# A hybrid layer on one core: another order of the mixers, compressed scores from a split key, and 128-column blocks without padding

## The chip, the core and the metric

The kernel runs on one core of a Trainium2 chip. The metric is the device time of one execution in microseconds; the kernel before took 1316.21 us as the median of 3 runs (1316.2 to 1316.97). Times in the profile are those of one profiled execution.

## What is computed

One transformer layer over a sequence of 1024 tokens of width 1024, in float32: an RMS norm, one input projection, four kinds of mixers on its columns, a gain per group, an output projection with a residual, a second norm and a gated feed-forward network.

```
proj = rms_norm(x) @ w_in
o_a = nsa_mixer(...)                  # 4 heads: compressed, selected and window attention, gated
o_b = gate_b * conv(gate_c * u)       # 256 channels, 3 taps
o_c = stick_breaking_attention(...)   # 4 heads: softplus, a reverse running sum, exp
o_d = dilated_attention(...)          # 4 heads: three dilations, mixed by their log-sums
groups = rms_norm([o_a, o_b, o_c, o_d]) * g_out
x = x + groups @ w_out
x = x + (silu(h2 @ w_gate) * (h2 @ w_up)) @ w_down      # h2 = rms_norm(x)
```

In the compressed branch the keys are reduced to 63 tokens, and a query block is scored against all 63 (`einsum('bhqd,bnd->bhqn', qi, kc)`).

## The kernel before

**Number format.** A float32 operand of a matmul is held as two tiles of type fp32r, a high part and the rest ("hi" and "lo", `whi` and `wlo`, `XH` and `XL`); a product is three matmuls (`mm3`, lines 240 to 243), or two where the high and low parts of one operand are stacked in the 128 rows. Where an operand stays plain float32 (the compressed scores, line 693, and transposes), one matmul is issued; the trace has two records for each such score matmul.

**Stages.** The normalized rows are transposed into `XH` and `XL`; keys and values are compressed (lines 454 to 508); then come the mixers, each of the letters in `ORDER` (line 44) being one piece of the program: `n0 n1` the two head pairs of the first mixer (`attn_nsa`, line 635), `c0 c1` the halves of the convolution (`conv`, line 806), `pd0 pd1` and `ps0 ps1` the projections for the dilated and stick-breaking attention (lines 379 and 385), `d0 d1` and `s0 s1` these attentions (`attn_dil`, line 738; `attn_stick`, line 775), and `g` (`gains`, line 832), which reads seven of the eight 128-row groups of mixed results back and scales them into `MH` and `ML`. The eighth group, that of the last attention, goes there straight from `finish` (line 622). After that `out_half` (line 899) multiplies by `w_out`: for rows 512 to 1023 with the seven groups alone, the eighth being added at the end (line 975), for rows 0 to 511 with all eight. The feed-forward network follows (lines 1042 to 1215), with products in a scheme of seven instead of eight.

**Attention.** Queries go in blocks of 128 rows (`qt`); scores are formed by `qk_pair` (line 513) over the keys up to the diagonal, in chunks of up to 512 columns. `chunks` (line 535) gives each chunk its width and the width it is run at: `res.append((c, w, max(256, w)))`, so that a chunk of 128 columns is run as 256 and half of the result is not used. A dilated or stick-breaking block then passes VectorE (the minimum with a bias, line 545, or the cap, lines 791 and 793, and the running sum, line 799), ScalarE and, in the stick-breaking case, GpSimd (line 801), before `pv` (line 568) transposes the probabilities on TensorE (line 580), takes them out of PSUM as hi and lo (`evac_T`, lines 564 and 565) and multiplies them with the values (lines 584 and 585). Two query blocks share these last matmuls, 256 columns; the last key block belongs to the second query block alone, and its matmul is filled up to 256 with 128 columns of zeros that stand at the head of each of the four buffers of `pt_pair` (line 550).

**What sets the order.** The program is built twice. The first time a planner (`_traced`, `_planned`) walks all instructions up to the last pools with a cost for each (`_duration`, line 1489) and starts on each engine the ready instruction that is first in the program, moved up by a lead; leads stand in a table by engine, tile tag and tile (`LEADS`, line 1244). The second time each engine's instructions, and the slots of the tiles, are pinned to that plan (`fix_order`, line 1768). So work of a later piece runs beside an earlier one, as far as tiles allow: the ring `QK` of smq has 10 tiles of 4 KB per partition (the keys and queries of the first mixer hold 8; each `pd` or `ps` takes 5), and the tag `V` has 2.

Of the kernel before, what the change touches and what calls it, by code (L numbers as in the profile page):

```python
# [9 lines left out]
F32 = mybir.dt.float32  # L10
# [6 lines left out]
T = 1024  # L17
# [26 lines left out]
ORDER = "n0 n1 c0 pd0 d0 pd1 d1 ps0 s0 c1 ps1 g s1".split()  # L44
# [7 lines left out]
def hybrid(ctx, tc, pools, x, gmix, wa1, wa2, wkv, wcv, wd, wc, bgate, gcols, pe, w1, w2,  # L52
# [393 lines left out]
    kcT = cst.tile([128, 64], F32, name="kcT")  # L446
# [7 lines left out]
    for z, src in ((0, KK), (1, VV)):  # L454
# [40 lines left out]
        if z == 0:  # L495
# [9 lines left out]
            nc.scalar.activation(kcT[:, :63], tp[:, :63], AF.Copy, scale=gsc[:, 1:2])  # L505
# [42 lines left out]
    PT = []  # L548

    def pt_pair():  # L550

        if not PT:
            for i in range(2):
                z = [sm.tile([128, 640], F32R, tag=f"pt{i}{c}", bufs=1, name=f"pt{c}") for c in "hl"]
                for t in z:
                    nc.gpsimd.memset(f(t[:, 0:128]), 0.0)
                PT.append(z)
        PT.reverse()
        return PT[0]

    def evac_T(tp, n):
        ph, pl = pt_pair()
        c = slice(128, 128 + n)
        nc.scalar.activation(ph[:, c], tp[:, :n], AF.Copy)  # L564
        nc.vector.tensor_tensor(pl[:, c], tp[:, :n], f(ph[:, c]), op=OP.subtract)  # L565
        return ph, pl

    def pv(o, items, first=True, last=True):

        n = len(items)  # L570
        for g in range(0, n, 2):
            tp = Ttile()
            grp = items[g:g + 2]
            cols = (128, 384)
            ps = [p for it in grp for p in it[:2]]
            if grp[-1][0] is None:
                cols = (256, 0)
                ps = [ps[3], ps[0], ps[1]]
# [22 lines left out]
    def finish(k8, c0, n, m, tmp, bank=None):  # L601
        nc.scalar.activation(tmp, m, AF.Square)
        for h in range(0, n, 512):
# [3 lines left out]
            if SQ == 0 or (SQ == 1 and k8 == 5):  # L607
                nc.tensor.matmul(ps[:, :w], f(blk1r), tmp[:, c], start=True, stop=True)
            else:
                sh, sl = (whl("sh"), whl("sl")) if bank else (z[:, 128:640] for z in pt_pair())  # L610
# [10 lines left out]
        if k8 == 5:  # L621
            gain(5, m, c0 // 512, slice(c0 % 512, c0 % 512 + n))
            return
# [11 lines left out]
    def attn_nsa(hp, Q):  # L635
# [7 lines left out]
        for qt in range(NT):  # L643
# [48 lines left out]
            for h in range(2):  # L692
                nc.tensor.matmul(ps[h][:, :63], f(Q[h][:, qc]), kcT[:, :63], start=True, stop=True)
# [8 lines left out]
            nc.tensor.matmul(o[:, :256], vcHL, ph[:, 128:384], start=True, stop=False)  # L702
            nc.tensor.matmul(o[:, :256], vcHL, pl[:, 128:384], start=False, stop=False)
# [118 lines left out]
    def gain(k, m, h, c):  # L822
        hi, lo = (z[:, k, c] for z in MS[h])
        if k != 5 and GP >> h & 1:
# [7 lines left out]
    def gains():  # L832
        flush_stores()
        MS.extend((xtile("MH"), xtile("ML")) for _ in range(2))
        if GH:
            for h in (1, 0):
                for k in (0, 1, 2, 3, 6, 7, 4):
# [3 lines left out]
        else:  # L841
            for k in (0, 1, 2, 3, 6, 7, 4):
# [6 lines left out]
    for o in ORDER:  # L849
        if o[0] == "c":  # L850
# [5 lines left out]
        else:  # L856
# [6 lines left out]
            else:  # L863
                if not i:
                    tri_ = [diag_mask()]
                attn_stick(i, *done["ps" + o[1]])
    att.close()
# [72 lines left out]
    K7 = ((0, 1, 2, 3, 6, 7, 4), ((0, 2), (2, 2), (6, 2), (4, 1)))  # L940
# [5 lines left out]
    out_half(0, (0, 1, 2, 3, 6, 7, 4, 5), ((0, 2), (2, 2), (6, 2), (4, 2)), range(0, D, 256))  # L946
# [13 lines left out]
    w5 = []  # L960
    for h in range(2):
        raw = wraw()
        nc.sync.dma_start(raw[:, :512], wout[:, 5, h * 512:(h + 1) * 512])
        hi, lo = whl("whi"), whl("wlo")
        split(hi[:, :512], lo[:, :512], raw[:, :512])
        w5.append((hi[:, :512], lo[:, :512]))
# [4 lines left out]
    for t in range(4, NT):  # L971
        c = slice(t % 4 * 128, t % 4 * 128 + 128)
        for h in range(2):
            ps = PRt()
            mm3(ps, tuple(z[:, 5, c] for z in MS[1]), w5[h], True, True)
# [115 lines left out]

    for i in range(NF // 2):
# [152 lines left out]
    "ACT B22 B": -430,  # L1245
    "ACT QK St": -535,
    "ACT QK ckh": -277,
    "ACT QK ckl": -96,
    "ACT QK cqh": -569,
    "ACT QK cql": -698,  # L1250
    "ACT QK dkh": -727,
    "ACT QK dkl": -1057,
    "ACT QK dqh": 921,
    "ACT QK dql": -192,
    "ACT QK er": -998,
    "ACT QK fw": -1315,
    "ACT QK ksh": 211,
    "ACT QK kt": 12,
    "ACT QK kwh": 629,
    "ACT QK q01h": -828,  # L1260
    "ACT QK q01l": -338,
    "ACT QK q23h": -732,
    "ACT QK q23l": 33,
# [6 lines left out]
    "ACT S4 S": 368,  # L1270
    "ACT S4 cm": 459,
    "ACT S4 kv": 1132,
    "ACT S4 wa": -119,
    "ACT T3 T": 286,
    "ACT T4 T": -754,
    "ACT V VA": -39,
    "ACT V VC": -861,
    "ACT V VD": -499,
    "ACT V bhl": -98,
    "ACT V yc": 297,  # L1280
    "ACT W R": -15,
    "ACT X B": 658,
    "ACT X MH": 74,
    "ACT X T": -744,
    "ACT X XH": -406,
    "ACT gt gt": 677,
    "ACT hss hss": 866,
    "ACT kcT kcT": -217,
    "ACT ll ll": -294,
    "ACT otmp otmp": 1259,  # L1290
    "ACT otmp tk": 109,
    "ACT pt0h pth": -106,
    "ACT pt1h pth": -55,
    "ACT pth pth": -53,
    "ACT pth sh": 6,
    "ACT ss ss": -37,
    "ACT tk raw": -981,
    "ACT tk rawk": 332,
    "ACT tk sq": -645,
    "ACT tk vraw": -340,  # L1300
    "ACT vcHL vcHL": 1499,
    "ACT whl c": -827,
    "ACT whl p": -826,
    "ACT whl sh": 66,
    "ACT whl u": -1188,
    "ACT whl whi": 97,
    "DVE B22 B": -223,
    "DVE MO MO": -290,
    "DVE QK St": -351,
    "DVE QK ckr": -103,  # L1310
    "DVE QK cqh": -1540,
    "DVE QK cql": 425,
    "DVE QK dkr": 192,
    "DVE QK dqh": -544,
    "DVE QK dql": -245,
    "DVE QK er": -357,
    "DVE QK fw": -2071,
# [554 lines left out]
```

## Time and profile before

| | before |
|---|---|
| median of 3 runs | 1316.21 us |
| the profiled execution | 1314.44 us |
| its span, first to last instruction | 1312.7 us |
| TensorE matmul busy | 1281.9 us |
| VectorE busy | 987.8 us |
| ScalarE busy | 703.9 us |
| GpSimd busy | 659.6 us |

The sum of the prediction is made against the profiled execution, 1314.44 us, which is 1.8 us below the median; 1.7 us of it lie outside of the span. Busy time of TensorE counts from each matmul's start to its modelled end, and neighbours overlap; the spacing of starts tells more than the durations. PEld is the load of the stationary operand, which runs beside the matmuls.

### The profile page before, as it was taken

How to read it: one execution, taken by the hardware profiler on the slowest of the kernel's cores; microseconds unless marked ns; L12 is line 12 of the kernel's file. 1: busy time of each engine (PE TensorE's matmuls, PEld its weight loads, DVE VectorE, ACT ScalarE, POOL GpSimd, SP SyncE). 2: the span in 40 equal slices, each digit the busy share in tenths (PEclk: the TensorE clock that was granted, in tenths of full speed). 3: DMA queues.
4: the chain of work that ended last, by engine and by line, in shares of the span. 5: the costliest groups of instructions: out<-in, count | busy, mean ns of one | idle time of the engine just before them, and what ended most of it. 6: DMA issues, size and time to landing. Idle time of an engine off the chain costs nothing.

```text
span 1312.7 us, 20252 instructions
## 1 busy us (share of the span) xinstructions
PE 1281.9 (98%) x7041; PEld 1089.3 (83%) x7041; DVE 987.8 (75%) x1792; ACT 703.9 (54%) x1437; POOL 659.6 (50%) x492
## 2 busy tenths in 40 slices
PE   8999999999999999999999999999999999999998
PEld 7988889999788887898987888888888887887886
DVE  5868888898878865885577979677765677499963
ACT  5658688777768875576554333332333335523440
POOL 6454256443214463786882446344543344564755
PEclk9999999999999999999999999999999999999999
DMA  7340021121312025533554454233232239862434
GB/s 249 93 125 12 5 79 40 41 75 28 100 49 60 11 66 148 165 120 117 161 190 144 156 189 153 84 118 120 101 107 73 93 124 321 283 198 73 145 97 152
DMA packets 90550, 153.04 MB, mean 117 GB/s; under 512 B 10128, under 2 KB 35728, under 8 KB 90448
## 3 DMA queue, kind: packets, MB, share of 16 engines
q1 hardware_dynamic: 89888, 149.92, 35.5%
q0 software_dynamic: 560, 1.84, 0.4%
q8 instruction: 55, 0.90, 0.3%
q14 instruction: 47, 0.39, 0.1%
HBM read 111.08 MB, written 36.44 MB: 112 GB/s over the span
## 4 chain that ended last, share of the span: by engine, by line
PE 79%; DVE 10%; DMA 4%; ACT 3%; issue 2%; POOL 1%; SPq 0%; DVEq 0%; POOLq 0%; ACTq 0%
PE PRp L241 9%; PE PRp L242 9%; PE PRp L243 9%; PE Tp L580 4%; PE PRp L1062 4%; PE PRp L1061 4%; PE PRp L1060 4%; PE SPp L518 2%; PE Op L585 2%; PE Tp L1060 2%; PE SPp L1060 2%; PE SPp L1061 2%; PE SPp L1062 2%; PE Tp L1061 2%; PE Tp L1062 2%
## 5 line engine op out<-in xcount | busy, mean ns | idle before, releaser
L108 POOL TENSOR_TENSOR wlo<-raw,whi 128x512 fp32r<-128x512 f32 x94 | 133.4, 1425 | 89.4 <-ACT whi L107 70.0
L1049 POOL TENSOR_TENSOR fw<-fraw,fw 128x512 fp32r<-128x512 f32 x50 | 72.0, 1441 | 137.9 <-ACT fw L1048 111.0
L565 DVE TENSOR_TENSOR ptl<-Tp,pth 128x512 fp32r<-128x512 f32 (+2 forms) x172 | 102.3, 605 | 26.8 <-ACT pth L564 23.7
L1119 DVE TENSOR_TENSOR fw<-sraw,fw 128x512 fp32r<-128x512 f32 x73 | 89.1, 1240 | 34.7 <-ACT fw L1118 34.6
L1048 ACT ACTIVATE fw<-fs 128x512 fp32r<-128x512 f32 x88 | 52.9, 629 | 112.9 <-DVE fs L1039 84.9
L564 ACT ACTIVATE pth<-Tp 128x512 fp32r<-128x512 f32 (+2 forms) x172 | 89.3, 530 | 44.3 <-PE Tp L580 30.2
L580 PE MATMUL Tp<-ident,S 128*128 128x128 f32 x552 | 101.5, 273 | 3.2 <-DVE ptl L565 3.1
L1119 POOL TENSOR_TENSOR hw<-bB,hw 128x512 fp32r<-128x512 f32 x55 | 80.4, 1476 | 46.6 <-ACT hw L1118 46.5
L241 PE MATMUL PRp<-XH,whi 128*128 128x512 f32 x224 | 90.5, 404 | 0.3 <-DVE VD L374 0.3
L242 PE MATMUL PRp<-XL,whi 128*128 128x512 f32 x224 | 90.0, 402 | 0.0
L243 PE MATMUL PRp<-XH,wlo 128*128 128x512 f32 x224 | 89.6, 400 | 0.0
L1049 DVE TENSOR_TENSOR fw<-fs,fw 128x512 fp32r<-128x512 f32 x88 | 76.4, 901 | 14.2 <-ACT fw L1048 14.0
L660 POOL TENSOR_SCALAR S<-S,ll 128x640 f32<-128x640 f32 (+7 forms) x32 | 53.8, 1680 | 63.1 <-DVE ll L658 14.4
L107 ACT ACTIVATE whi<-raw 128x512 fp32r<-128x512 f32 x102 | 63.0, 619 | 33.7 <-PE PRp L242 13.3
L580 PEld LDWEIGHTS Tp<-ident,S 128*128 128x128 f32 x552 | 69.1, 141 | 10.3 <-DVE ptl L565 3.9
L241 PE MATMUL PRp<-whi,MH 128*128 128x256 f32 (+1 forms) x248 | 71.3, 291 | 1.0 <-ACT MH L827 0.6
L242 PE MATMUL PRp<-wlo,MH 128*128 128x256 f32 (+1 forms) x248 | 71.3, 289 | 0.0
L243 PE MATMUL PRp<-whi,ML 128*128 128x256 f32 (+1 forms) x248 | 70.5, 289 | 0.0
L801 POOL TENSOR_TENSOR S<-S,R 128x128 f32<-128x128 f32 (+7 forms) x32 | 47.5, 1484 | 42.9 <-DVE R L799 42.9
L1048 ACT ACTIVATE fw<-fraw 128x512 fp32r<-128x512 f32 x50 | 31.3, 627 | 68.5 <-PE PRp L1062 35.0
L1118 ACT ACTIVATE hw<-bB 128x512 fp32r<-128x512 f32 x62 | 38.8, 628 | 53.0 <-PE Op L243 24.6
L1039 POOL TENSOR_TENSOR u<-u,p 128x512 f32<-128x512 f32 x22 | 32.5, 1478 | 64.7 <-DVE u L1039 43.9
(472 smaller groups left out, 4504.2 us busy)
## 6 DMA issues: line engine op xcount, KB each, us to landing
fraw<-in_wgate_dram SPq DMA_DIRECT2D x22, 512.0 KB, 3.9
fraw<-in_wup_dram SPq DMA_DIRECT2D x22, 512.0 KB, 4.3
bB<-in_wdown_dram SPq DMA_DIRECT2D x44, 256.0 KB, 4.3
sraw<-hS SPq DMA_DIRECT2D x44, 256.0 KB, 2.7
raw<-in_wout_dram SPq DMA_DIRECT2D x30, 256.0 KB, 2.8
hS<-s SPq DMA_DIRECT2D x30, 256.0 KB, 2.2
sraw<-hA SPq DMA_DIRECT2D x29, 256.0 KB, 3.9
xt<-in_x_dram SPq DMA_DIRECT2D x8, 512.0 KB, 9.6
```

The costliest lines, as they stand in the source:

```text
L108: (lo or nc.gpsimd).tensor_tensor(dst_lo, raw, f(dst_hi), op=OP.subtract)
L241: nc.tensor.matmul(ps, a[0], b[0], start=first, stop=False)
L242: nc.tensor.matmul(ps, a[0], b[1], start=False, stop=False)
L243: nc.tensor.matmul(ps, a[1], b[0], start=False, stop=last)
L564: nc.scalar.activation(ph[:, c], tp[:, :n], AF.Copy)
L565: nc.vector.tensor_tensor(pl[:, c], tp[:, :n], f(ph[:, c]), op=OP.subtract)
L580: nc.tensor.transpose(tp[:, i * 128:(i + 1) * 128], p, ident)
L1049: eng.tensor_tensor(wt[:, 1, :], a, f(wt[:, 0, :]), op=OP.subtract)
L1060: nc.tensor.matmul(ps, wt[:, 0, c], bh[:, k, :], start=k == 0, stop=False)
L1061: nc.tensor.matmul(ps, wt[:, 0, c], bl[:, k, :], start=False, stop=False)
L1062: nc.tensor.matmul(ps, wt[:, 1, c], bh[:, k, :], start=False, stop=k == 3)
L1119: eng.tensor_tensor(wt[:, 1, :], raw, f(wt[:, 0, :]), op=OP.subtract)
```

## The change

- `ORDER` becomes `n0 c0 n1 c1 ps0 s0 ps1 s1 pd0 d0 pd1 g d1`. The last attention, whose group goes straight into `MH` and `ML`, is `d1` instead of `s1`; the numbers 5 and 7 of the groups change places accordingly in `finish`, `gain`, `gains`, `K7` and the group that is added at the end.
- The compressed keys become two fp32r tiles, and a compressed score is two matmuls of 64 columns instead of one float32 matmul of 63.
- `chunks` runs a chunk at its own width. `pv` multiplies the last key block at 128 columns; the zeros and their four memsets go, and `pt_pair` is a plain ring of 2 per tag.
- The planner has another table of leads, now by tile and by tile and stage (`pools.mark()` marks the beginning of each piece), and counts 400 ns instead of 60 for each DMA issue of SP. So the order on every engine, up to the last pools, is another one, and the SP and POOL queues with it.

```diff
-ORDER = "n0 n1 c0 pd0 d0 pd1 d1 ps0 s0 c1 ps1 g s1".split()
+ORDER = "n0 c0 n1 c1 ps0 s0 ps1 s1 pd0 d0 pd1 g d1".split()
...
-    kcT = cst.tile([128, 64], F32, name="kcT")
+    kcT = [cst.tile([128, 64], F32R, name=f"kcT{c}") for c in "hl"]
+    for z in kcT:
+        nc.gpsimd.memset(f(z[:, 63:64]), 0.0)
...
-            nc.scalar.activation(kcT[:, :63], tp[:, :63], AF.Copy, scale=gsc[:, 1:2])
+            nc.scalar.activation(kcT[0][:, :63], tp[:, :63], AF.Copy, scale=gsc[:, 1:2])
+            nc.vector.scalar_tensor_tensor(kcT[1][:, :63], tp[:, :63], gsc[:, 1:2], f(kcT[0][:, :63]),
+                                           op0=OP.mult, op1=OP.subtract)
...
-            res.append((c, w, max(256, w)))
+            res.append((c, w, w))
...
-                z = [sm.tile([128, 640], F32R, tag=f"pt{i}{c}", bufs=1, name=f"pt{c}") for c in "hl"]
-                for t in z:
-                    nc.gpsimd.memset(f(t[:, 0:128]), 0.0)
-                PT.append(z)
-        PT.reverse()
-        return PT[0]
+        return [sm.tile([128, 512], F32R, tag=f"pt{c}", bufs=2, name=f"pt{c}") for c in "hl"]
...
-            if grp[-1][0] is None:
-                cols = (256, 0)
-                ps = [ps[3], ps[0], ps[1]]
+            ps = [p for it in grp for p in it[:2] if p is not None]
...
-                c = slice(cols[i], cols[i] + 256)
-                nc.tensor.matmul(o[:, :256], v, ph[:, c], start=first and g + i == 0, stop=False)
-                nc.tensor.matmul(o[:, :256], v, pl[:, c], start=False, stop=last and g + i == n - 1)
+                b = 256 if grp[i][0] is not None else 128
+                c = slice(i * 256, i * 256 + b)
+                nc.tensor.matmul(o[:, 256 - b:256], v, ph[:, c], start=first and g + i == 0, stop=False)
+                nc.tensor.matmul(o[:, 256 - b:256], v, pl[:, c], start=False, stop=last and g + i == n - 1)
...
-        if k8 == 5:
-            gain(5, m, c0 // 512, slice(c0 % 512, c0 % 512 + n))
+        if k8 == 7:
+            gain(7, m, c0 // 512, slice(c0 % 512, c0 % 512 + n))
...
-                nc.tensor.matmul(ps[h][:, :63], f(Q[h][:, qc]), kcT[:, :63], start=True, stop=True)
+                for i in range(2):
+                    nc.tensor.matmul(ps[h][:, :64], Q[h][:, qc], kcT[i], start=i == 0, stop=i == 1)
...
-    K7 = ((0, 1, 2, 3, 6, 7, 4), ((0, 2), (2, 2), (6, 2), (4, 1)))
+    K7 = ((0, 1, 2, 3, 4, 5, 6), ((0, 2), (2, 2), (4, 2), (6, 1)))
...
-        return 60
+        return 400 if outs else 60
...
-        op.lead = sum(EARLIER[k] for k in op.kinds) + (LEADS.get(op.group, 0) if acc else 0)
+        op.stage = f"{op.group} @{sum(m <= op.n for m in marks)}"
+        op.lead = sum(EARLIER[k] for k in op.kinds)
+        if acc:
+            op.lead += LEADS.get(op.group, 0) + LEADS.get(op.stage, 0)
```

## Rows read from the trace of the kernel before

**Rows 1.** Part 1 of the page: engine, busy us (share of the span), instructions, and the span.

```profile
span 1312.7 us, 20252 instructions
PE 1281.9 (98%) x7041; PEld 1089.3 (83%) x7041; DVE 987.8 (75%) x1792; ACT 703.9 (54%) x1437; POOL 659.6 (50%) x492
```

**Rows 2.** Busy time by stretch. Columns: from:to and length in us; busy us (instructions) of PE, PEld, DVE, ACT, POOL; granted TensorE clock; DMA share; GB/s. The stretches from 99 to 610 us are, by the first and last instructions of their tiles, n0 and n1; d0 and most of d1; the rest of d1 with s0; and s1.

```profile
75.00:100.00 25.00, 22.18 (x159) 19.28 (x157) 13.61 (x27) 15.15 (x33) 17.23 (x13) 1.00 0.42 126
99.00:284.00 185.00, 182.70 (x1245) 163.17 (x1244) 160.21 (x584) 142.56 (x370) 91.50 (x77) 1.00 0.13 39
284.00:393.00 109.00, 107.46 (x715) 95.50 (x714) 89.30 (x225) 80.52 (x181) 24.48 (x20) 1.00 0.22 61
393.00:512.00 119.00, 116.95 (x630) 98.07 (x628) 84.58 (x131) 85.80 (x159) 52.36 (x39) 1.00 0.25 72
512.00:610.00 98.00, 91.25 (x676) 84.71 (x677) 78.43 (x119) 64.87 (x117) 70.11 (x43) 0.98 0.40 121
700.00:1080.00 380.00, 379.51 (x1627) 304.90 (x1626) 281.56 (x338) 126.53 (x218) 165.75 (x112) 1.00 0.36 121
1080.00:1110.00 30.00, 28.96 (x126) 23.25 (x125) 22.95 (x32) 15.41 (x26) 13.03 (x14) 1.00 0.86 302
1200.00:1225.00 25.00, 23.15 (x99) 18.19 (x98) 23.36 (x24) 13.54 (x25) 18.46 (x12) 1.00 0.37 112
```

**Rows 3.** Waits of PE and of SP in 475 to 625 us: who waited for whom, us in total, times, longest.

```profile
PE Op L584 <- ACT pth L564: 2.2, 3, 1.0
...
SPq L131 <- POOL wlo L108: 67.7, 27, 8.1
```

**Rows 4.** The timeline of TensorE in the first mixer: start us, us, instruction (those in a row merged).

```profile
181.07 0.28 PE L585 MATMUL Op<-ptl,VA 128*128 128x256 f32 x1
181.18 0.28 PE L584 MATMUL Op<-pth,VA 128*128 128x256 f32 x1
181.30 0.28 PE L585 MATMUL Op<-ptl,VA 128*128 128x256 f32 x1
181.41 0.28 PE L584 MATMUL Op<-pth,VA 128*128 128x256 f32 x1
181.53 0.28 PE L585 MATMUL Op<-ptl,VA 128*128 128x256 f32 x1
181.65 0.60 PE L580 MATMUL Tp<-ident,S 128*128 128x128 f32 x4
```

**Rows 5.** The timeline of the loads of the stationary operand a little later, around compressed scores of 63 columns.

```profile
186.18 0.30 PEld L693 LDWEIGHTS SPp<-kcT,q23l 128*128 128x128 f32 x2
186.40 0.19 PEld L518 LDWEIGHTS SPp<-ksh,q23h 128*128 128x128 f32 x1
186.51 0.19 PEld L520 LDWEIGHTS SPp<-ksl,q23h 128*128 128x128 f32 x1
```

**Rows 6.** Groups of TensorE by line and shape: count | busy us, mean ns | idle before.

```profile
L580 PE MATMUL Tp<-ident,S 128*128 128x128 f32 x552 | 101.5, 273 | 3.2 <-DVE ptl L565 3.1
L693 PE MATMUL SPp<-kcT,q23h 128*128 128x63 f32 x16 | 2.7, 250 | 0.0
```

**Rows 7.** Groups of VectorE in 75 to 625 us: count | busy us, mean ns | idle before and releaser.

```profile
L565 DVE TENSOR_TENSOR ptl<-Tp,pth 128x512 fp32r<-128x512 f32 (+2 forms) x172 | 102.3, 605 | 26.8 <-ACT pth L564 23.7 <-POOL wlo L108 1.8
L799 DVE TENSOR_TENSOR_SCAN R<-one,R 128x128 f32<-128x128 f32 (+7 forms) x32 | 52.7, 1651 | 5.8 <-ACT R L798 5.4
L591 DVE TENSOR_TENSOR MO<-Op,otmp 64x128 f32<-64x128 f32 (+1 forms) x64 | 22.4, 350 | 9.0 <-ACT otmp L589 7.4
L791 DVE TENSOR_SCALAR S<-SPp 128x512 f32<-128x512 f32 (+3 forms) x40 | 20.8, 522 | 5.4 <-PE Tp L580 3.4 <-PE SPp L520 2.0
L620 DVE TENSOR_TENSOR MO<-MO,tk 128x256 f32<-128x256 f32 x24 | 16.5, 686 | 3.1 <-ACT tk L619 2.8
L793 DVE SCALAR_TENSOR_TENSOR S<-SPp,tri 128x128 f32<-128x128 f32 x32 | 8.9, 283 | 2.3 <-PE SPp L520 2.0
L299 DVE TENSOR_TENSOR raw<-raw,hss 128x512 f32<-128x512 f32 x12 | 8.6, 724 | 1.0 <-POOL hss L98 1.0
L296 DVE TENSOR_REDUCE hss<-sq 128x8 f32<-128x512 f32 x12 | 8.2, 682 | 3.5 <-ACT sq L294 3.5
L312 DVE SCALAR_TENSOR_TENSOR dqh<-PRp,gsc,dqh 64x512 fp32r<-64x512 f32 x4 | 3.0, 744 | 0.3 <-ACT dqh L311 0.2
L374 DVE TENSOR_TENSOR VD<-PRp,VD 128x512 fp32r<-128x512 f32 x4 | 2.8, 689 | 0.8 <-ACT VD L373 0.8
L545 DVE CUSTOM_DVE_ANT_0 Sc<-SPp,wct 128x63 f32<-128x63 f32 x32 | 6.8, 216 | 2.8 <-PE Tp L700 2.5
```

**Rows 8.** GpSimd in s1 (512 to 610 us) and its memsets of the zeros: duration ns min/median/max, first and last start.

```profile
L108 POOL TENSOR_TENSOR wlo<-raw,whi 128x512 fp32r<-128x512 f32 (+1 forms) x18 | 30.8, 1712 | 18.7 <-ACT whi L107 11.5 <-issue 2.9 <-PE PRp L242 2.8
L801 POOL TENSOR_TENSOR S<-S,R 128x256 f32<-128x256 f32 (+7 forms) x15 | 23.2, 1546 | 5.7 <-DVE R L799 5.7
...
L556 POOL MEMSET ptl<- x2: 197/200/204, 0.9 to 1.4; 128x128 f32 x2
```

**Rows 9.** The stretch of s1 in which the granted clock fell, columns as in rows 2.

```profile
535.50:539.00 3.50, 3.50 (x14) 2.70 (x13) 3.44 (x5) 1.21 (x3) 1.38 (x2) 0.53 0.61 198
```

**Rows 10.** The timeline of TensorE just before that: start us, us, instruction, and in brackets the idle time before it and what ended it.

```profile
534.35 0.38 PE L584 MATMUL Op<-pth,VC 128*128 128x256 f32 x1 [1.03 <-ACT pth L564]
```

**Rows 11.** Part 6 of the page: a load of 512 KB by SP: count, KB each, median us from issue to landing.

```profile
xt<-in_x_dram SPq DMA_DIRECT2D x8, 512.0 KB, 9.6
```

More of the change, by code (lines that the diff above doesn't have):

```diff
@@ new lines @@
+    "ACT S4 wa @0": 98,
+    "ACT T3 T": 1048,
+    "ACT T3 T @14": -807,
+    "ACT T4 T": -1988,
+    "ACT T4 T @14": 1327,
+    "ACT V VA": 30,
+    "ACT V VC": -1919,
+    "ACT V VC @5": -90,
+    "ACT V VC @7": 288,
+    "ACT V VD": -939,
+    "ACT V VD @11": -197,
+    "ACT V VD @9": 299,
+    "ACT V bhl": 199,
+    "ACT V bhl @0": 157,
+    "ACT V yc": 416,
+    "ACT V yc @2": -143,
+    "ACT V yc @4": 63,
+    "ACT W R": -41,
+    "ACT W R @6": 135,
+    "ACT W R @8": -16,
+    "ACT X B": 2397,
@@ new lines @@
+    "ACT X B @14": 1059,
+    "ACT X MH": -68,
+    "ACT X MH @13": -680,
+    "ACT X T": -1624,
+    "ACT X T @14": -63,
+    "ACT X XH": -417,
+    "ACT X XH @0": -97,
+    "ACT gt gt": 606,
+    "ACT gt gt @0": 27,
+    "ACT hss hss": 1415,
+    "ACT hss hss @0": -41,
+    "ACT kcT kcT": -343,
+    "ACT kcTh kcTh": 176,
+    "ACT kcTh kcTh @0": -242,
+    "ACT ll ll": -385,
+    "ACT ll ll @1": -155,
+    "ACT ll ll @13": 331,
+    "ACT ll ll @3": -30,
+    "ACT otmp otmp": 1588,
+    "ACT otmp otmp @1": -104,
@@ new lines @@
+    "ACT whl whi @5": 442,
+    "ACT whl whi @7": -53,
+    "ACT whl whi @9": -763,
+    "DVE B22 B": -768,
+    "DVE B22 B @14": -929,
+    "DVE MO MO": -250,
+    "DVE MO MO @1": -12,
+    "DVE MO MO @10": -3,
+    "DVE MO MO @13": 12,
+    "DVE MO MO @3": -26,
+    "DVE QK St": -609,
+    "DVE QK St @0": -960,
+    "DVE QK ckr": 913,
+    "DVE QK ckr @5": 290,
+    "DVE QK ckr @7": 256,
+    "DVE QK cqh": -1764,
+    "DVE QK cqh @5": 42,
+    "DVE QK cqh @7": 371,
+    "DVE QK cql": 1734,
+    "DVE QK cql @5": 221,
@@ new lines @@
+    "DVE V VC @7": -71,
+    "DVE V VD": 345,
+    "DVE V VD @11": -252,
+    "DVE V VD @9": 260,
+    "DVE V bhl": -367,
+    "DVE V bhl @0": -183,
+    "DVE V yc": 334,
+    "DVE V yc @2": -350,
+    "DVE V yc @4": -1,
+    "DVE W R": 1862,
+    "DVE W R @6": -96,
+    "DVE W R @8": 141,
+    "DVE W xn": -1380,
+    "DVE W xn @0": 195,
+    "DVE X ML": 364,
+    "DVE X ML @12": 55,
+    "DVE X ML @13": -144,
+    "DVE X T": -2513,
+    "DVE X T @14": 319,
+    "DVE X XL": 128,
+    "DVE X XL @0": -254,
@@ new lines @@
+    "DVE blk1r blk1r": 19,
+    "DVE blk1r blk1r @0": -895,
+    "DVE car car": -9,
+    "DVE df df": -305,
+    "DVE df df @14": -675,
+    "DVE df fs": -944,
+    "DVE df fs @15": -26,
+    "DVE epst epst": -1998,
+    "DVE epst epst @0": -211,
+    "DVE gates gates": -1125,
+    "DVE gates gates @0": 100,
+    "DVE gsc gsc": 257,
+    "DVE gsc gsc @0": 451,
+    "DVE gt gt": -1343,
+    "DVE gt gt @0": 254,
+    "DVE half half": 4019,
+    "DVE half half @0": -282,
+    "DVE hss hss": -2719,
@@ new lines @@
+    "DVE hss hss @0": 23,
+    "DVE hss hss @11": -597,
+    "DVE hss hss @9": -682,
+    "DVE ident ident": -971,
+    "DVE ident ident @0": -408,
+    "DVE kcTl kcTl": -163,
+    "DVE kcTl kcTl @0": 452,
+    "DVE ll ll": -45,
+    "DVE ll ll @10": 462,
+    "DVE ll ll @13": -193,
+    "DVE mm mm": 14,
+    "DVE mm mm @1": -35,
+    "DVE mm mm @10": 4,
+    "DVE mm mm @13": -5,
+    "DVE mm mm @3": -2,
+    "DVE nt nt": 489,
+    "DVE nt nt @14": -99,
+    "DVE one1 one": -2197,
+    "DVE one1 one @0": -313,
@@ new lines @@
+    "DVE whl u @15": -17,
+    "DVE whl wlo": 117,
+    "DVE whl wlo @0": 286,
+    "PE O Op": -18,
+    "PE O Op @0": -112,
+    "PE O Op @10": -212,
+    "PE O Op @13": 20,
+    "PE O Op @15": 3,
+    "PE O Op @6": 7,
+    "PE O Op @8": -6,
+    "PE PR PRp": 6,
+    "PE PR PRp @0": 9,
+    "PE PR PRp @10": -138,
+    "PE PR PRp @11": -4,
+    "PE PR PRp @13": -10,
+    "PE PR PRp @14": -6,
+    "PE PR PRp @2": 343,
+    "PE PR PRp @4": 45,
+    "PE PR PRp @5": 107,
+    "PE PR PRp @7": 36,
+    "PE PR PRp @9": -140,
@@ L1399 @@
[L1399 to L1417 removed]
+    "POOL S4 S": -356,
+    "POOL S4 S @1": 86,
```

620 lines of the change are left out of this document (422 added, 198 removed).

## The prediction

> **What bounds it now.** I read part 1 of the page first: TensorE is busy for 1281.9 of 1312.7 us, and the next engine, VectorE, for 987.8 [rows 1]. So there are 30.8 us in which TensorE does nothing, and a change can only pay through the time of TensorE's own work or through such holes. The busy time by stretch says where these are [rows 2]. The feed-forward network is full: 1627 matmuls of 512 columns in 380 us are 233.6 ns each, start to start, and that price has no slack. In the mixers the idle time is 2.3 us of 185 for n0 and n1, 1.5 of 109 for most of the dilated attention, 2.05 of 119 around s0, and 6.75 of 98 around s1: s1 is the stage that leaks. VectorE is at 87% there for n0 and n1 (160.2 of 185), at 82%, 71% and 80% in the others. So one engine, TensorE, sets the time nearly everywhere, and VectorE is the one that makes it wait when a stage has too little of other TensorE work beside its attention. The waits agree: around s1 TensorE waits for the hi and lo parts of probabilities [rows 3].
>
> **The 128-column blocks.** Counted in the code: the score chunks with 128 columns left over are those of block 0 in both branches of the first mixer (8 matmuls per head pair, 16) and of blocks 0 and 4 of the dilated and of the stick-breaking attention (8 per head pair, 16 and 16); the last key block of `pv` is 64 matmuls. Together 112 matmuls fall from 256 to 128 columns. A matmul of 256 columns takes 117 ns from start to start (181.07 to 181.53 in four steps) [rows 4]. No row has an fp32r matmul of 128 columns. The nearest rows say that the stationary operand sets a floor: four transposes of 128 columns span 0.60 us and the last lasts 0.273, so they come every 109 ns [rows 4, 6]; and around compressed scores of 63 columns, with half of the columns again, the loads still start 110 ns apart (186.18 to 186.40 for two, then 186.51) [rows 5]. Each of the 112 matmuls loads another operand. I take 109 ns: 112 x -8 ns = -0.9 us. The ends: half of 117, if the floor is not one for fp32r, 112 x -58.5 = -6.6 us; and 233.6 ns, what four times 128 columns cost, if a short fp32r matmul runs in four passes as plain float32 does, 112 x +116.6 = +13.1 us.
>
> A rule of the Trainium skill would have it otherwise: the page "TensorE: Matmul & The Clock Gate", section "Back-to-back issue gap", gives 134 cycles at full clock for 128 columns, which would be 56 ns, 61 less than the 117, or -6.8 us in all. The 109 and 110 ns of the rows speak against it.
>
> **The compressed scores.** 32 float32 matmuls, 64 records in the trace [rows 6], become 64 fp32r matmuls of 64 columns: as many operand loads as before. At the floor of 110 ns this is 0. Ends: 56 ns less each without the floor, -3.6 us; 4 x 64 columns at the rate of 256, 117 ns, +0.4. The new VectorE instruction on 63 columns takes some 0.22 us by its nearest row [rows 7]; the values are compressed after the keys and cover it, and without that cover it costs 0.22. The four memsets of 0.2 us that go run in the first 2 us, the two that come have one column: 0 [rows 8].
>
> **The order.** Each attention has other TensorE work beside it, as far as the tile rings allow. Counted with 233.6, 117 and 109 ns, a projection piece or half of the convolution is 144 matmuls of 512 columns or their like, 33.7 us, and a pair of heads of s or d by itself 26.1: 8.9 for 48 score matmuls, 9.4 for 80 value matmuls, 7.8 for 72 transposes. VectorE needs for one s 58.8 us: half of 52.7, 20.8 and 8.9 for lines 799, 791 and 793, 20 x 0.605, 8 x 0.35 and 4 x 0.686 for lines 565, 591 and 620 [rows 7]. The dilated pair has no running sum and nothing on GpSimd between.
>
> What moves: at the end stands d1 in place of s1, with the same `out_half` beside it. s1 there shares GpSimd with the weights of `out_half`: 23.2 us of line 801 and 30.8 of line 108, and SP stands 67.7 us before loads whose buffer waits for line 108 [rows 3, 8]. d1 leaves GpSimd to these weights. If the last stage idles like the dilated one now, 1.4% of 98 us, 5.35 of 6.75 us come back: **-5.3**. After such a hole (1.03 us before a value matmul, among others [rows 10]) the granted clock was 0.53 for 3.5 us, between the levels of 1.2 and 2.4 GHz and nearly all at the lower [rows 9]; that is 0.47 x 3.5, and without the hole **-1.6**. Ends for both: 0, and the whole 6.75 + 1.6. To SP's queue d1 brings two bias loads of 512 KB, which s1 has not; the query copies go with either. They are issued before `g` and the DMA engines are 40% busy there [rows 2], so 0; if they come late, once a landing, 9.6 us [rows 11].
>
> The price is paid in the middle. s1 now runs with `pd0` beside it: `pd1` needs 5 tiles of the ring that s1 holds. TensorE's work there is 26.1 + 36.3 (`pd0` with its 24 transposes) = 62.4 us, VectorE's 58.8 + 13.0 (4 x 0.72 and 4 x 0.68, 8 x 0.75, 2 x 0.69 for `pd0` [rows 7]) = 71.8. VectorE is the longer by 9.4 us. Most of that can be shifted: s0, with `c1` and `ps1`, has more TensorE than VectorE work, and n0 and n1 show that 87% of VectorE goes with 1.2% of idle TensorE [rows 2]. I take the idle time of the nearest stage, that around s0, once more: **+2.0**. Ends: 0, and 71.8 / 0.87 - 62.4 = +20. For n0 and n1, which get `c0` and part of `ps0` where they had `c0` and part of `pd0`, 0; what is queued on SP moves with its stage. A step later than planned holds up what is behind it on its engine, since each engine's order is pinned.
>
> **The plan.** With other leads, and 400 ns per DMA issue, nearly every queue is reordered; no row prices that. From below it is bounded by the idle time that is left in the mixers (2.3 + 1.5 + 2.05), before them (2.8) and in the network's two holes (1.04 and 1.85), -11.5 us [rows 2]; from above by a whole mixer part as leaky as s1, 6.9% of 511 us against 12.6, +22.6. I take 0: nothing in the rows says which.
>
> **The sum.** -0.9 + 0 - 5.3 - 1.6 + 2.0 + 0 = -5.8 us against the profiled execution's 1314.4, so 1308.6; the median stands 1.8 higher, so 1310.4, and I say **1310**.
>
> **Rivals.**
> 1. *s1 starves in the middle.* The place is s1 beside `pd0`, the price a hole between the 9.4 us that VectorE is longer and the 20 at its highest observed share, so 15, in place of my 2: -5.8 - 2 + 15 = +7, 1323. It decides for slower from a hole of 10.4 us on. For it: the scan's waits and 71.8 against 62.4 us. Against: the 1.2% of idle time at 87% of VectorE in n0 and n1. Chance 0.20.
> 2. *Short fp32r matmuls take four passes.* +13.1 in place of -0.9, and +0.4 for the scores: +8.6, 1325. For it: no fp32r matmul under 256 columns is in the trace, so nothing excludes it. Against: plain float32 scores of 63 columns already come at 110 ns. Chance 0.09.
> 3. *No floor by the operand load.* -6.6 and -3.6 in place of -0.9 and 0: -15, 1301. By it the skill's rule above would hold. The transposes, which are plain float32, may be slow for another reason. Chance 0.09.
> 4. *The change does nothing measurable*: the tail's gain is given back in the middle one for one, within 2.6 us of the median. Chance 0.14.
> 5. *The new plan closes other holes too*, half of the 11.5: about 1305. Chance 0.07.
>
> My forecast itself has 0.40; 0.01 is left for what I have not named. Faster by over 0.2% (2.6 us, about what a measurement of this kernel can tell from none): 0.40 + 0.09 + 0.07 = 0.56. Within: 0.14. Slower: 0.20 + 0.09 + 0.01 = 0.30. The likeliest sign's own range is 1299 to 1313; since both signs hold much, the range for 8 in 10 goes from 1297 (rival 3 with part of rival 5) to 1326 (rivals 1 and 2).
>
> **What would show it.** Step one: loads of the stationary operand stay near 110 ns apart at the 128-column value matmuls; 55 would be rival 3, starts 230 apart rival 2. Step two: the stage with d1 and `out_half` idles near 1.4% with the clock at 1.00, and GpSimd's weights are no longer late. Step three: the stretch of s1 with `pd0` idles some 2 us; over 10 is rival 1, with waits for lines 565, 799 or 801 before TensorE. The feed-forward network stays at 233.6 ns per matmul. I am wrong if the tail is no tighter, if the hole turns up in the middle, or if the plan opens holes in n0 and n1.

## The result, and the profile after

| | before | after |
|---|---|---|
| median of the runs made side by side | 1316.2 us (4 runs) | 1306.49 us (4 runs, 1303.94 to 1307.19) |
| the profiled execution | 1314.44 us | 1303.94 us |
| its span | 1312.7 us | 1302.1 us |

The ratio is 0.9921, 95% interval 0.9905 to 0.9937: 10 us less, where 6 were forecast. One trace below, that of the run with all three cuts, is of a slow execution, 54 us above the median of its run and late only from 700 us on, so it is read up to 610 us. Part 1 of the page after, against [rows 1]:

```profile
span 1302.1 us, 20263 instructions
PE 1276.2 (98%) x7041; PEld 1086.6 (83%) x7041; DVE 977.5 (75%) x1793; ACT 701.9 (54%) x1437; POOL 654.5 (50%) x490
```

The count of matmuls is the same, since the float32 score already had two records, and every engine's work is nearly as before. The span fell by 10.6 us, the busy time of TensorE by 5.7, so the other half came out of TensorE's idle time. Where, the busy time by stretch says; columns as in [rows 2]. The stretches are the stages of the new order: the end of the start, n0 and n1 with the convolution, s0, s1, d0, d1 beside `out_half`, and 23 us of `out_half` behind d1's last value matmul; then the network and its two holes, and last the place where the clock falls now.

```profile
75.00:100.00 25.00, 22.69 (x157) 20.14 (x156) 14.21 (x29) 14.85 (x33) 16.45 (x12) 1.00 0.37 108
100.00:292.00 192.00, 189.80 (x1169) 164.62 (x1169) 161.94 (x579) 141.10 (x361) 91.57 (x78) 0.99 0.12 38
292.00:357.00 65.00, 64.20 (x352) 53.28 (x351) 55.55 (x90) 54.36 (x101) 34.49 (x25) 1.00 0.19 51
357.00:432.00 75.00, 72.09 (x502) 64.72 (x502) 66.90 (x103) 65.75 (x125) 43.56 (x29) 1.00 0.14 38
432.00:494.00 62.00, 60.58 (x450) 56.37 (x448) 51.67 (x124) 49.38 (x108) 20.50 (x16) 1.00 0.31 87
494.00:577.00 83.00, 79.07 (x577) 72.60 (x576) 68.73 (x148) 55.31 (x120) 34.07 (x27) 1.00 0.46 145
577.00:600.00 23.00, 23.00 (x196) 23.00 (x196) 6.19 (x11) 8.57 (x18) 10.90 (x9) 1.00 0.51 161
700.00:1075.00 375.00, 375.00 (x1606) 301.20 (x1605) 268.32 (x328) 124.17 (x214) 165.28 (x112) 1.00 0.35 120
1070.00:1100.00 30.00, 28.42 (x124) 22.79 (x123) 23.37 (x33) 16.07 (x27) 13.96 (x15) 1.00 0.87 315
1190.00:1215.00 25.00, 24.22 (x104) 19.24 (x103) 23.13 (x25) 12.42 (x23) 16.06 (x12) 1.00 0.37 107
...
162.00:167.00 5.00, 4.27 (x18) 3.43 (x17) 3.49 (x11) 2.49 (x7) 4.81 (x4) 0.66 0.00 0
```

Read the stretches with attention for the idle time, length minus the first figure: the last stage has 3.93 us (83.00 less 79.07), and the 23 us after it none, where s1 had 6.75 of 98; s1 in the middle has 2.91 of 75.

A busy TensorE is not a full one, so I also priced each matmul by the start-to-start spacing of its width where matmuls follow each other closely (512 columns 233.6 ns, 384 175, 268 122, 256 117, 128 and less 109) and took the sum from the length of each stretch. I call the remainder *lost*: holes, a lower clock and wider spacing together. It is that of one execution on either side.

| lost, us | before | after | difference |
|---|---|---|---|
| start, 0 to 100 | 17.2 | 14.7 | -2.5 |
| n0 and n1 | 11.5 | 8.8 | -2.7 |
| the two middle pairs of heads and the third | 9.8 (284 to 512) | 12.2 (292 to 494) | +2.4 |
| the last stage | 13.5 (512 to 610) | 8.0 (494 to 577) | -5.5 |
| rest, to the last matmul's start | 5.0 | 3.8 | -1.2 |
| needed work at these prices | 1251.2 | 1250.2 | -1.0 |

The sum is -10.5 us. Lost time is more than idle time: n0 and n1 idled for 2.3 us before (185.00 less 182.70 [rows 2]) and for 2.2 after, so the 2.7 us that they lose less lie inside TensorE's busy time, in closer spacing. What made it closer stays open; the widths there are another mix, too. The network kept its 233.6 ns per matmul (375 us for 1606 records).

### The profile page after: what moved, and what is told of

Its sections match the earlier page's. It is cut to its first block, busy times and chain, and to the rows that moved or that the text cites. A ratio compares the mean times of both kernels' runs of the same rounds, so it can differ in the third digit from the quotient of the medians.

```text
span 1302.1 us, 20263 instructions
## 1 busy us (share of the span) xinstructions
PE 1276.2 (98%) x7041; PEld 1086.6 (83%) x7041; DVE 977.5 (75%) x1793; ACT 701.9 (54%) x1437; POOL 654.5 (50%) x490
## 4 chain that ended last, share of the span: by engine, by line
PE 85%; DVE 7%; DMA 2%; ACT 2%; issue 2%; POOL 1%; SPq 0%; DVEq 0%; POOLq 0%; ACTq 0%
PE PRp L241 11%; PE PRp L243 10%; PE PRp L242 10%; PE Tp L570 4%; PE PRp L1056 4%; PE PRp L1054 4%; PE PRp L1055 4%; PE SPp L522 3%; PE SPp L1056 2%; PE Tp L1056 2%; PE SPp L1054 2%; PE Tp L1054 2%; PE SPp L1055 2%; PE Tp L1055 2%; PE Op L575 2%; PE SPp L524 2%
## 5 line engine op out<-in xcount | busy, mean ns | idle before, releaser
L108 POOL TENSOR_TENSOR wlo<-raw,whi 128x512 fp32r<-128x512 f32 x94 | 129.4, 1385 | 84.9 <-ACT whi L107 56.2
L570 PE MATMUL Tp<-ident,S 128*128 128x128 f32 x552 | 94.0, 275 | 1.2 <-DVE S L651 0.7
L1043 DVE TENSOR_TENSOR fw<-fs,fw 128x512 fp32r<-128x512 f32 x88 | 71.9, 846 | 14.8 <-ACT fw L1042 14.7
L570 PEld LDWEIGHTS Tp<-ident,S 128*128 128x128 f32 x552 | 67.7, 141 | 11.5 <-DVE ptl L559 1.4
L1042 ACT ACTIVATE fw<-fraw 128x512 fp32r<-128x512 f32 x50 | 31.4, 627 | 69.9 <-PE Tp L1056 18.1
```

The source lines that it names most:

```text
L108: (lo or nc.gpsimd).tensor_tensor(dst_lo, raw, f(dst_hi), op=OP.subtract)
L570: nc.tensor.transpose(tp[:, i * 128:(i + 1) * 128], p, ident)
L1043: eng.tensor_tensor(wt[:, 1, :], a, f(wt[:, 0, :]), op=OP.subtract)
```

## Experiments

In all of them but the five with a new plan, the order of every engine is pinned to that of the kernel which they start from: the edit acts only when the program is built the second time, and the extracts of code leave out the switch for that. Ratios are to runs of before made beside them; 0.001 is 1.3 us.

### What 128 columns cost

**Padding put back** in the changed kernel, order kept. In each filled-up value matmul the added columns are those of the neighbouring block, whose sums are thereby changed.

```diff
-            res.append((c, w, w))
+            res.append((c, w, max(256, w)))
...
+                if b == 128:
+                    b, c = 256, slice(i * 256 - 128, i * 256 + 128)
```

> The changed kernel with its order on every engine and its tile slots kept as they are, and the 128-column blocks run at 256 columns again: 120 matmuls (in the last key block the added columns are a block of probabilities once more, so those attention outputs are not the reference's). Theory (the load of the stationary operand sets a floor of 110 ns): +1.0 us, ratio to the changed kernel 1.0007, 256-column starts 117 ns apart. Rival (no floor, 58 ns at 128 columns): +7 us. Rival (four passes at 128): -14 us.

Measured: 1308.84 us, ratio 0.9942 (0.9927 to 0.9957), so 2.8 us above the changed kernel by the ratios, with intervals of 2 us on either. Four passes are out. Between the floor's +1.0 and no floor's +7 it stands nearer the floor, but does not decide alone: its trace has a fall of the clock at 83 us that the changed kernel's has not, and loses 18.1 us in the start instead of 14.7, before any block is run.

**Twice the number of 128-column matmuls**: in the changed kernel every value matmul of 256 columns, but those that begin a sum, is issued as two of 128 (488 more instructions).

```diff
-                nc.tensor.matmul(o[:, 256 - b:256], v, pl[:, c], ...)
+                for q in range(2):
+                    nc.tensor.matmul(o[:, q * 128:q * 128 + 128], v, pl[:, c.start + q * 128:c.start + q * 128 + 128], ...)
```

> The changed kernel with order and slots kept, and 488 value matmuls of 256 columns each issued as two of 128 with the same stationary operand. Theory (each matmul pays its operand load, 110 ns at least): +488 x 103 ns = +50 us. Rival (no floor): about 0 to +1 us. Rival (four passes): +170 us.

Measured: 1350.51 us in a single execution, 44.0 above the changed kernel's median: 90 ns for each added matmul, where no floor asks 0 and the floor 101 (2 x 109 - 117). The timeline of TensorE in this run, two matmuls to a line:

```profile
300.61 0.39 PE L584 MATMUL Op<-pth,VA 128*128 128x128 f32 x2
300.83 0.39 PE L584 MATMUL Op<-ptl,VA 128*128 128x128 f32 x2
301.06 0.39 PE L584 MATMUL Op<-pth,VA 128*128 128x128 f32 x2
301.28 0.39 PE L584 MATMUL Op<-ptl,VA 128*128 128x128 f32 x2
301.50 0.39 PE L584 MATMUL Op<-pth,VA 128*128 128x128 f32 x2
```

Eight matmuls from 300.61 to 301.50: 111 ns each, hardly less than for 256 columns. So there is a floor. That the load of the operand makes it, and not some other cost of each matmul, is argued and not shown: every matmul here loads an operand. In the changed kernel itself it is easy to misread, because such a pair stands between wider matmuls. Its timeline:

```profile
447.49 0.28 PE L576 MATMUL Op<-ptl,VC 128*128 128x256 f32 x1
447.60 0.23 PE L575 MATMUL Op<-pth,VC 128*128 128x128 f32 x1
447.67 0.27 PE L576 MATMUL Op<-ptl,VC 128*128 128x128 f32 x1
447.77 0.45 PE L241 MATMUL PRp<-XH,whi 128*128 128x512 f32 x1
448.06 0.39 PE L242 MATMUL PRp<-XL,whi 128*128 128x512 f32 x1
```

The first of the pair seems to take 70 ns, the second 100; the next, of 512 columns, then takes 290 instead of 233.6. The starts run ahead and the wide matmul pays for it: 460 ns for the three against 2 x 109 + 233.6 = 452. The loads of their operands keep 110 to 120 ns, which is what the prediction wanted to see there:

```profile
447.49 0.19 PEld L575 LDWEIGHTS Op<-pth,VC 128*128 128x128 f32 x1
447.61 0.19 PEld L576 LDWEIGHTS Op<-ptl,VC 128*128 128x128 f32 x1
447.72 0.19 PEld L241 LDWEIGHTS PRp<-XH,whi 128*128 128x128 f32 x1
447.83 0.19 PEld L242 LDWEIGHTS PRp<-XL,whi 128*128 128x128 f32 x1
```

### The last stage of before

What held TensorE up beside s1? The prediction blamed s1's chain and the GpSimd that it shares with the weights of `out_half`. Three things in that stage were cut, first one by one; the work on the weights (line 108) was not.

**s1's running sum cut short** (64 elements; the rest of each sum is left out), in before and, as a control, in the changed kernel.

```diff
-  nc.vector.tensor_tensor_scan(R[:, ::-1], ..., R[:, ::-1], ...)
+  m = 64 if hp == 1 else L
+  nc.vector.tensor_tensor_scan(R[:, :m][:, ::-1], ..., R[:, :m][:, ::-1], ...)
```

> The kernel before with its order and slots kept, and the running sum of s1 done over 64 columns only (its output is not the reference's): some 26 us of VectorE work less in the tail stage. Theory (the hole of the tail is s1's chain through VectorE and GpSimd): idle time of TensorE around s1 falls from 6.75 us towards 1.5 to 2.5 and the fall of the clock there goes, -5 to -7 us, 1309 to 1311. Rival (the hole is made by the gathering of the seven groups and by the output weights): less than 2 us.

Measured: 1314.09 us, ratio 0.9981 (0.9969 to 0.9994), -2.5 us. VectorE fell from 78.43 [rows 2] to 57.70 us in the stretch:

```profile
512.00:610.00 98.00, 92.23 (x691) 86.24 (x690) 57.70 (x119) 67.52 (x121) 60.40 (x44) 0.98 0.42 123
```

Only 1 us of TensorE's idle time went, the stretch lost 12.0 us where before's lost 13.5, and the clock still fell near 537. So the sum on VectorE alone is not the cause.

> The changed kernel with order and slots kept and the running sum of s1 over 64 columns only, now in the middle beside pd0. Theory (s1 there runs short of TensorE work, VectorE at 89% sets part of it): the stretch from 357 to 432 us gets 2 to 4 us shorter. Rival (TensorE's work alone sets that stretch): less than 1 us.

Measured: 1305.28 us, ratio 0.9913 (0.9894 to 0.9931): with s1 in the middle its chain costs about 1 us, inside the interval.

**Late loads and GpSimd.** A closer look at before shows two other engines late at the same moment. ScalarE, whose queue holds the gains (L827) in front of s1's exponential, stood for two loads that SP had issued only when a buffer came free:

```profile
529.79 0.72 ACT L827 ACTIVATE MH<-gm,go 128x512 fp32r<-128x512 f32 x1 [2.68 <-DMA gm<-mixd]
...
532.55 0.72 ACT L827 ACTIVATE MH<-gm,go 128x512 fp32r<-128x512 f32 x1 [1.00 <-DMA gm<-mixd]
```

And GpSimd ran four gains in a row ahead of s1's product (L801):

```profile
521.79 0.74 POOL L801 TENSOR_TENSOR S<-S,R 128x256 f32<-128x256 f32 x1
522.51 7.26 POOL L825 TENSOR_SCALAR MH<-gm,go 128x512 fp32r<-128x512 f32 x4
529.75 0.94 POOL L801 TENSOR_TENSOR S<-S,R 128x256 f32<-128x256 f32 x1
```

First the loads alone were taken out of the way: the last two chunks read the buffer of the fifth.

```diff
                 nc.sync.dma_start(m, mixd[k])
+                if k in (7, 4):
+                    m = m6            # the buffer of k == 6
```

> The kernel before with the order of every engine kept; the gains of the last two of the seven mixer chunks read the fifth chunk's buffer instead of the two loads that are issued last (the loads still run, their data are not used), so no gain waits for them. Theory (late loads): ScalarE's in-order queue stands 2.68 and 1.00 us for these two loads in the s1 stretch of before, the eviction and the exponential that TensorE waits for stand behind it, and the fall of the clock at 535.7 us follows from the holes: 2 to 4 us less than before, and no fall of the clock near 536 us. Rival (s1's own chain is as late as the loads): the same holes under another name, less than 1 us either way, and the clock falls as before.

Measured: 1316.17 us, ratio 1.0004 (0.9993 to 1.0016): nothing. The rival holds. The same place in ScalarE's timeline now reads (line numbers are one higher here):

```profile
532.37 0.42 ACT L803 ACTIVATE S<-S 128x256 f32<-128x256 f32 x1 [2.88 <-POOL S L802]
```

The wait has passed on to the product on GpSimd, 2.88 us for 2.68. The fall of the clock in this stage did go, and bought nothing even there: the stretch lost 14.1 us. This execution has falls at 80 to 90 us (0.68) and near 1207 us that before's has not; the run with the short sum has the first of them and that near 537 as well. Then the seven gains of GpSimd went to ScalarE as well:

```diff
-        if k != 5 and GP >> h & 1:
+        if False:                     # in the second build
```

> The kernel before with the order of every engine kept, the gains of the last two mixer chunks reading the fifth chunk's buffer (as in the run without the late loads), and the seven gains that GpSimd did now done by ScalarE at the same places. Theory: the hole of the s1 stretch near 530 to 534 us is the product of s1 and the gains on one GpSimd queue, where four gains of 7.3 us stand ahead of s1's product; with both waits gone TensorE's holes there (0.58, 0.74, 1.03 us) and the fall of the clock go: 2 to 5 us less than before. Rival (the wait passes on, to ScalarE, which now does 7 x 0.72 = 5.0 us more, or to VectorE): within 1.5 us of before.

Measured: 1314.06 us, ratio 0.9983 (0.9970 to 0.9995), -2.2 us. It is the lower edge of the theory, and its trace does not bear out the mechanism: TensorE idles as long in the stretch as before (6.88 us by the first row below, against 6.75), and what went is the fall of the clock. (Its profiled execution is 2.6 us above the median.) Last, all three cuts together:

> The kernel before with the order of every engine kept and the three earlier cuts at the s1 stretch together: s1's scan 64 elements long instead of 384 or more, no gain waiting for the two late loads, the gains off GpSimd. If the cuts add (they gave -2.1, +0.6 and -1.8 us alone): 3 to 5 us less than before, and TensorE's lost time in the stretch 512 to 610 falls from 13.5 to about 10 us. If s1 beside the gains is all of what the last stage costs more than d1 in the changed kernel: 5 us or more and 8 us lost, as there. Rival (the holes have one cause elsewhere, the order of TensorE itself): no more than the best cut alone, -2 to -2.5 us, and 12 us lost.

Measured: 1312.72 us, ratio 0.9974 (0.9961 to 0.9986), -3.4 us. By the ratios the parts alone were -2.5 and -2.2, together -4.7; the interval, -1.8 to -5.1, holds that sum and the better part alone. The stretch of s1 with the gains off GpSimd, and with all three:

```profile
512.00:610.00 98.00, 91.12 (x680) 84.21 (x679) 78.84 (x118) 69.68 (x124) 57.52 (x36) 1.00 0.41 127
```

```profile
512.00:610.00 98.00, 93.83 (x720) 88.69 (x721) 56.82 (x120) 72.30 (x130) 52.19 (x40) 1.00 0.39 122
```

Idle 6.88 and then 4.17 us, the latter near the 3.93 of the changed kernel; lost 12.7 and then 8.3, against 13.5 before and 8.0 there. (Its earlier stretches lose nearly what those of before do, 17.2, 11.2, 5.4 and 4.7 us.) So in this one execution the three cuts together took 5.2 us off the stretch, where the sum alone took 1.5 and the other two together 0.8. That fits three chains that are late together, each hiding the others: the running sum on VectorE, the loads ahead of ScalarE's queue, and the gains ahead of s1's product on GpSimd. The median, which gained 3.4 us, neither confirms nor excludes it. Not tested are the sum with one of the other two cuts, and the weights on GpSimd, which the prediction named.

### Order, blocks and plan apart

Here the planner made a new plan each time.

**The new order alone**, with the old instructions, leads and costs (the numbers of the groups change with it, which the extract leaves out):

```diff
-ORDER = "n0 n1 c0 pd0 d0 pd1 d1 ps0 s0 c1 ps1 g s1".split()
+ORDER = "n0 c0 n1 c1 ps0 s0 ps1 s1 pd0 d0 pd1 g d1".split()
```

> The kernel before with the new order of the mixers alone (and the gain chunks that go with it), blocks still padded to 256 columns, scores in float32, the planner's leads and costs as before; the plan is made anew. If the order carries the gain, as the predicted terms have it (tail -5.3, middle +2.0, clock -1.6): 1308 to 1313 us. Rival, the plan that was fitted to this order carries it: 1316 us or more, with the time lost in n, the starts or the first s stage rather than in the tail.

Measured: 1330.31 us, ratio 1.0110 (1.0093 to 1.0127): the expectation for an order that carries the gain fails, and the rival, 1316 us or more, holds. It placed the loss outside of the tail, though, and the last 83 us up to d1's last value matmul leak too:

```profile
514.00:597.00 83.00, 75.68 (x533) 67.91 (x534) 70.24 (x150) 55.92 (x121) 29.44 (x22) 0.98 0.44 144
```

TensorE idles for 7.32 us and loses 15.6 in them, where the changed kernel's last stage idles for 3.93 and loses 8.0 and that of before, with s1, 6.75 and 13.5. GpSimd is as free as in the changed kernel (29.44 us busy, there 34.07). So d1 at the end does not tighten the tail by itself.

**Blocks and split key alone** (those hunks of the change), in the old order with the old leads:

> The kernel before with the unpadded 128-column blocks and the split key for the compressed scores alone, in the old order of the mixers and with the old leads and costs; the plan is made anew. By the predicted terms (blocks -0.9, scores 0): 1315 to 1316 us. Four passes for 128 columns: +12 or more. Rival, the old leads do not fit the changed instructions: the blocks' microsecond is drowned in a new plan's holes, 1318 us or more, or 1311 or less if the new plan is luckier.

Measured: 1336.35 us, ratio 1.0162 (1.0140 to 1.0185): a change that needs 1 us less work cost 21. TensorE waits in 480 to 500 us of that run, at the end of s0, beside `c1`:

```profile
483.20 0.38 PE L576 MATMUL Op<-ptl,VC 128*128 128x256 f32 x1 [1.75 <-DVE ptl L559]
485.11 0.50 PE L606 MATMUL PRp<-sh,blk1r 128*128 128x512 f32 x1 [1.35 <-ACT sh L605]
486.81 0.58 PE L606 MATMUL Tp<-pth,blk1r 128*128 128x256 f32 x1 [1.20 <-ACT pth L605]
...
495.87 0.38 PE L575 MATMUL Op<-pth,VC 128*128 128x256 f32 x1 [1.08 <-ACT pth L558]
```

**The changed kernel without its leads by stage:**

```diff
-            op.lead += LEADS.get(op.group, 0) + LEADS.get(op.stage, 0)
+            op.lead += LEADS.get(op.group, 0)
```

> The changed kernel without the leads by stage in its planner; the plan is made anew. If the order itself carries the gain, 1306 to 1309 us. If the fitted plan does (the unpredicted 5 us at the starts and in n0, n1), 1310 to 1316 us, with the loss in the starts and the n stages.

Measured: 1327.18 us, ratio 1.0089 (1.0074 to 1.0104), 20.7 us above the changed kernel and beyond both expectations. The leads by tile were left as they stand beside those by stage, so this is what leaving out a part of the table costs, and not what leads by stage are worth.

**The cost of a transfer in the plan**, 400 ns in before and 60 in the changed kernel:

```diff
-        return 400 if outs else 60
+        return 60
```

> The kernel before with one planner cost alone changed (a transfer that SP issues is taken as 400 ns instead of 60) and the plan made anew; same instructions, same order of the mixers. If an unfitted plan costs what the others did: 1325 to 1336 us, and 25 us or more lost by TensorE over the last two pairs of mixers. If that cost is a repair by itself: 1316 us or less.

Measured: 1317.82 us, ratio 1.0013 (1.0000 to 1.0027).

> The changed kernel with the planner's cost of a transfer that SP issues set back from 400 to 60 ns and the plan made anew. Any plan that the leads were not fitted to: 1320 to 1335 us. If the plan is robust, within 3 us of the changed kernel. If the new order is better whatever the plan, TensorE loses less in the last pair of mixers than in the unfitted plans of the old order (31 us there), 12 to 20 us.

Measured: 1306.94 us, ratio 0.9928 (0.9911 to 0.9945). Both expectations of a large effect were wrong: this cost is worth some 1 to 2 us, and the two plans lose nearly what those they came from do, which shows that not every new plan is a bad one. What TensorE lost, worked out as above, one execution each. The stretches end at 100 us, at the first score matmul of the third and of the fifth pair of heads, and at the last value matmul; what comes after is in the total alone:

| lost, us | start | n0, n1 | next two pairs | last two pairs | total |
|---|---|---|---|---|---|
| before (old order, its leads) | 17.2 | 11.4 | 5.5 | 17.8 | 57.0 |
| the same, cost of 400 ns | 17.4 | 11.3 | 5.4 | 17.2 | 58.0 |
| blocks alone (old order, leads of another program) | 18.8 | 20.9 | 4.3 | 30.8 | 83.9 |
| after (new order, its leads) | 14.7 | 9.2 | 7.9 | 11.9 | 47.5 |
| the same, cost of 60 ns | 16.0 | 9.4 | 8.2 | 13.0 | 51.7 |
| after without stage leads | 22.2 | 10.5 | 16.7 | 17.7 | 71.7 |
| order alone (new order, old leads) | 19.7 | 16.7 | 4.8 | 24.4 | 74.4 |

Two things are to be seen. Compared at like fit, the new order loses less in the last two pairs (11.9 and 13.0 against 17.8 and 17.2; 17.7 and 24.4 against 30.8). In the two before them it loses more with its own leads (7.9 and 8.2 against 5.5 and 5.4) or without a part of them (16.7), but not with the old ones (4.8 against 4.3). And a plan whose leads do not belong to its program loses 24 to 27 us more than the one whose leads do, 21 to 24 by the medians, mostly in the mixers and the start. With the old table each of the change's two edits costs time. No table was made that fits one of them alone, so what each is worth by itself stays open.

## Why the prediction was right, and where it was not

- **Bound by TensorE: right.** But for 1.0 us of work, all of the gain is in TensorE's idle time, clock and spacing.
- **Blocks, -0.9: right.** The needed work fell by 1.0; it was 120 matmuls and not 112, since block 4 of the selected branch also has a chunk of 128 columns. Four steps from 181.07 to 181.53 are 115 ns and not 117, which would make the term -0.7 and changes nothing else. A floor of 111 ns is shown by the split run. Rival 3 (no floor) falls with it, and rival 2 (four passes), which would have cost +13.1. The Trainium skill's page "TensorE: Matmul & The Clock Gate", section "Back-to-back issue gap", gives the 134 cycles for 128 columns, 56 ns at the full clock, for an isolated matmul; for a stream of pairs of load and matmul, which this kernel is, the same section gives about 81 ns. The prediction took the first figure alone; the runs show 111 ns, above both.
- **Scores, 0: right.** The 64 records took 5.9 us, start to start, in either kernel.
- **Tail, -5.3, and clock, -1.6: near in size, the reason not borne out.** The last stage lost 5.5 us less in all, the vanished fall of the clock included, where the two terms made 6.9; its idle time fell by 2.8 and not to 1.4% (3.93 of 83 us is 4.7%). d1 does leave GpSimd free, 34.07 us busy of 83 where it was 70.11 of 98. But the weights are hardly less late. The 67.7 us of [rows 3] are SP's wait for them over 150 us; over the last stage alone the same view has, before (512 to 610 us) and after (494 to 577 us):

```profile
SPq L131 <- POOL wlo L108: 45.8, 15, 8.1
SPq L131 <- POOL wlo L108: 32.8, 10, 12.9
```

  That is 47% of the stage before and 40% after, and the longest wait has grown. With the old leads d1 at the end leaks like s1 did, GpSimd free or not (7.32 us idle). So the order alone does not give the term; it comes with the leads. Of what made s1 late the prediction named s1's two steps and the shared GpSimd, and not that the gains stood in front of s1 on two queues whose order is pinned. Apart from a fall in the first 20 us that both traces have, the clock fell once in each: before at 535 [rows 9], after at 163, behind a hole of 0.73 us in n0. Over 162 to 167 us it was 0.66, which is 0.34 x 5 = 1.7 us: the term is 0 and not -1.6.
- **Middle, +2.0: right.** Lost +2.4, idle 2.91 us in s1's stretch. Rival 1 (s1 starves, +15) needs a hole of over 10 us; VectorE at 89% there (66.90 of 75) was fed by other work, as the row of n0 and n1 had suggested. It is a matter of the plan, though: without the stage leads the two pairs lose 16.7 us, with the old table 4.8.
- **Plan, 0: the step that failed.** "I take 0: nothing in the rows says which" was -6.4 us (-2.5 in the start, -2.7 in n0 and n1, -1.2 in the rest). In number that is rival 5, "half of the 11.5: about 1305", and 1306.5 is nearer to that than to 1310. In mechanism it is not: the 11.5 were holes, and of those in the same places (75 to 100 us, n0 and n1, the network's two) only 1.1 us went, 8.0 to 6.9. The rest lies before 75 us, which the bound left out, and inside TensorE's busy time. The runs show why the term should have been wide and not absent: leaving out the leads by stage costs 20.7 us, and either edit with the old leads is 15 to 21 slower than before. Neither profile has a fall of the clock at 80 to 90 us, so the -2.5 in the start is not that; but other executions of the same starts do have one, see below.

Numbered against the parts, -1.0 for blocks, -5.5 for the tail with its clock, +2.4 for the middle and -6.4 for the plan make the -10.5 measured. The sign is in part luck. The prediction's terms for the order, -5.3, -1.6 and +2.0, should have held for the new order with the old leads too, and that run is 15 us slower than before; what made the change faster is an order with a table of leads made for it, for which the prediction had no row and no price.

## What to carry to other kernels

Where each engine's order is pinned by a plan, an edit and its plan are one change: price the plan by what idle time is left in every stage, and do not judge an edit by the time that it gives with the old plan (here +15 and +21 us for two edits that with leads of their own gained 10 together). Before blaming one chain for a hole, look at what stands late on each engine at that moment: if two or three are late together, cutting one can move the wait and little else, as the 2.68 us that became 2.88 show. Compare waits over stretches of like length and like place. Cutting columns below the spacing at which operand loads come (here 256 to 128, 117 to 111 ns) saved 1 us of work over 120 matmuls, while each matmul that was added cost 90 ns.

## What the runs showed of the hardware

- **The lower clock falls at other places for the same instructions.** The start of before and of the run without the late loads is the same program in the same order; over 80 to 90 us the granted clock was 1.00 in the one and 0.68 in the other, and the first 100 us lost 17.2 and 18.8 us. Of the runs with the start of the changed kernel, the padded one had such a fall there and lost 18.1, the changed kernel had none and lost 14.7. So up to 3 us between two single executions may be this, and a term of 1.6 us for one fall is within it.
- **A narrow matmul may start early and the next wide one pays**, as in the pair at 447.60 us: 70 and 100 ns, then 290 for a matmul that takes 233.6 elsewhere. Spacings of single matmuls are not prices; those of a run of like ones (111 ns over eight) are.
